# Attention query tiles, low products' chunks and attention output loaded earlier in a hybrid encoder block

## The chip, the cores and the metric

The kernel runs on one core of a Trainium2 chip. The core's engines are TensorE (PE in the profile: matrix products into PSUM, the matmul accumulators), VectorE (DVE), ScalarE (ACT), GpSimd (POOL) and SyncE (SP, which here only issues transfers); transfers between device memory and the on-chip SBUF run on 16 DMA engines, and their issues stand in the instruction queue of SP or POOL in program order. The metric is the time of one execution in microseconds (us) on the device; less is better.

## The reference

One layer for 1024 tokens of width 1024, all in float32:

```python
h = rms_norm(x, norm_mix)
proj = h @ w_in                    # q, k, v | rwkv columns | gates
attn = windowed_gqa(rope(norm(q)), rope(norm(k)), v, sink)   # 8 heads, 2 kv heads, +-128 tokens
zr = zr + shift_mu * (centred_shift(zr) - zr)
rw = rwkv7_time_mix(zr, ...)       # 8 heads of 64, one forward and one backward scan, summed
gates = sigmoid(proj[..., O_GATE:])
merged = gates[0] * (attn @ w_up_attn) + gates[1] * (rw @ w_up_rwkv)
x = x + merged @ w_out
x = x + square(relu(rms_norm(x, norm_ffn) @ w_ff1)) @ w_ff2
x = x + (p @ w_ple) * sigmoid(rms_norm(x, norm_ple) @ w_ple_gate)
```

In the scan each head holds a 64x64 state that is updated token by token with state·w + (state·a) b^T + v k^T; the output is state·r.

## The kernel before

Every float32 product of the large kind is made of three matmuls: each operand is split into a high part (a cast on ACT, line 198) and a low part (a subtraction on DVE or POOL, line 199), and high·high, low·high and high·low are summed. `split` does this, `mm3_steps` issues the three matmuls, one a step.

The work runs in stages. From 0 to 100 us: norm and the q, k, v projections (q and k go to device memory, `qT_d`, `kT_d`). From 100 to 280 us: the preparation of the scan in four channel groups of 128 (p = 0..3) and two directions; decay and in-context-rate products (`low_rank`, with the weights `wlr_h[0]`, `wlr_h[1]`, `wlr_l`), and the results written out as `ra_d`, `bk_d` (operands in chunks of 64 tokens), `v_d` and `bv_d` (the bonus term, tile `bv`, made from the PSUM tile `px`). From 280 to 340 us: the gate products of the first 512 tokens (`gates0`, tiles `gmm`: 16 gates of 24 matmuls) fill PE; their weights come as tiles `wst` on SP. From 340 to 476 us: windowed attention in 8 blocks of 128 queries (scores `sc`, transposes `pt`, outputs `po`, written to `at_d`), with the rest of gates0 as filler of low priority. From 476 to about 770 us: the scan, 16 steps of 64 tokens in both directions at once; then the up-projections, `w_out`, the FFN and the last embedding product, which the change does not touch.

A scan step s needs its operands (`rac`, `bkc`), its values (`UV`), the chunk products `gps` (`products`, evicted by DVE into the tile `gm`), sums (`sps`, `wy`, `ups`, `wa`) and transposes (`tmps`). Steps come in blocks of four. For each block a 64x64 triangular matrix per head and chunk has to be inverted: `low_products` loads pieces `la`, `lb` of `ra_d` and `bk_d` for its four chunks and multiplies them (`lps`); DVE then runs 31 pairs of vector operations (`inverse_steps`, tiles `tmp` and `Z`) to `Zn`, and PE turns the result into the inverse with `qps`. All this for block b+1 takes place during block b. The four chunks of low products are called in the first step of a block, one at each of four places; each call loads the chunk after it.

The scan's matmuls are issued in the order of the code (`mmo` pins it). Between them stand gaps: `fill(n)` takes n steps from one stream of filler, `beside()`: first the gate products of the last 512 tokens (`gates(1, ...)`), then the attention's up-projection (`uaps`: 8 groups of 12 matmuls for each half of the tokens), for which the attention output `at_d` is loaded (tile `atl`) and split into `aTh` and `aTl`. Between the two streams of filler stand `BRIDGE` = 26 empty steps, in which a gap issues nothing. Ahead of the scan a scheduler orders the matmuls by priority; it also places DMA issues on SP and POOL, and a pool of tiles that reuses the room of an earlier pool makes its first writers wait for that pool's last users.

SBUF room is handed from stage to stage: the attention's own pool `A2` opens on room that the preparation has used, and its query tiles `qT` (POOL, line 899), band masks `band` (line 903) and `sink` (line 905) are loaded there.

## Time and profile before

| | |
|---|---|
| three runs | 1707.08, 1701.10, 1699.73 us; median 1701.10 |
| the profiled execution | 1696.2 us, its span 1694.4 us |
| PE busy | 1615.2 us (95%) |
| DVE, ACT, POOL busy | 1138.1, 847.0, 103.1 us |
| mean granted TensorE clock | 0.982 of full speed |
| DMA | 269.23 MB, mean 159 GB/s |

The profile is a page on one execution and a trace that can be asked for more. A wait row reads: engine, tile and line that waited, what released it, then the total in us, the times and the longest. A window row gives the length, the busy time of PE, PE's weight loads, DVE, ACT and POOL with the number of instructions, then the granted TensorE clock (1.00 is full speed), the busy share of the DMA engines and GB/s. A row of the chain or of the timeline gives the start, the duration, the engine and the line; in brackets stands the idle time before it and what ended it. A row of groups gives line, engine, operation, tiles and count, then the total, the mean in ns, and the idle time before them.

### The profile page before, as it was taken

The page shows a single profiled execution, that of the slowest core. Times are in us where ns is not written, and L with a number is a line of the kernel's source. Part 1 is how long each engine was busy: PE and PEld are TensorE (multiplying, and loading weights), DVE is VectorE, ACT ScalarE, POOL GpSimd, SP SyncE. Part 2 cuts the span into 40 slices and gives each one's busy share as a digit, 9 for nine tenths or more (in the row PEclk, how much of TensorE's full clock was granted, in tenths as well). Part 3 has the DMA queues.
Part 4 walks back from the last instruction along what each step waited for, and adds up shares of the span by engine and source line. Part 5 has one row for each costly group of instructions (what it writes and reads, how often), then busy time and mean ns, then how long its engine had stood idle before and what let it go on. Part 6 is the DMA issues. An engine that isn't in the chain of part 4 may idle for free.

```text
span 1694.4 us, 31186 instructions
## 1 busy us (share of the span) xinstructions
PE 1615.2 (95%) x12280; PEld 1311.1 (77%) x12280; DVE 1138.1 (67%) x2055; ACT 847.0 (50%) x1537; POOL 103.1 (6%) x113
## 2 busy tenths in 40 slices
PE   7999999989999999698999999999999999999998
PEld 7987777856667787565778878888888888888887
DVE  6648998255948686775854887666767867685342
ACT  5558887357754544365423455444445444554121
POOL 3430000321200000000000000000000000000000
PEclk9999999989999999799999999999999999999999
DMA  6363556755366554446652154444449865574110
GB/s 222 82 154 106 161 172 174 229 171 152 104 181 182 159 162 129 154 150 217 232 195 95 55 174 150 155 147 164 143 150 345 286 200 166 155 219 145 41 41 38
DMA packets 200834, 269.23 MB, mean 159 GB/s; under 512 B 47728, under 2 KB 103920, under 8 KB 200688
## 3 DMA queue, kind: packets, MB, share of 16 engines
q1 hardware_dynamic: 190752, 254.14, 47.3%
q0 software_dynamic: 9792, 12.59, 2.9%
q8 instruction: 96, 1.57, 0.4%
q10 hardware_dynamic: 144, 0.52, 0.1%
q14 instruction: 50, 0.41, 0.1%
HBM read 186.45 MB, written 80.74 MB: 158 GB/s over the span
## 4 chain that ended last, share of the span: by engine, by line
PE 74%; DVE 11%; DMA 6%; ACT 4%; issue 3%; POOL 1%; SPq 0%; DVEq 0%; ACTq 0%; POOLq 0%
PE ff2ps L1856 17%; PE ff1ps L1604 16%; PE gmm L221 4%; PE uaps L221 2%; PE plps L231 2%; PE plps L229 2%; PE plps L227 2%; PE mm L239 2%; PE mm L241 2%; PE mm L240 2%; PE gps L221 1%; DMA wst<-in_w_col_dram 1%; DMA g1t<-g_d 1%; PE mmo L241 1%; PE mmo L239 1%
## 5 line engine op out<-in xcount | busy, mean ns | idle before, releaser
L1856 PE MATMUL ff2ps<-tl,sh 128*128 128x512 f32 x448 | 174.5, 389 | 0.1
L1856 PE MATMUL ff2ps<-th,sl 128*128 128x512 f32 x448 | 174.4, 389 | 0.0
L1856 PE MATMUL ff2ps<-th,sh 128*128 128x512 f32 x448 | 174.0, 389 | 0.0
L198 ACT CAST sh<-sst 128x512 fp32r<-128x512 f32 x109 | 67.7, 622 | 106.4 <-PE ff2ps L1856 59.9
L199 DVE TENSOR_TENSOR sl<-sst,sh 128x512 fp32r<-128x512 f32 x109 | 75.2, 690 | 46.5 <-ACT sh L198 46.1
L1604 PE MATMUL ff1ps<-mh,w1h 128*128 128x512 f32 x256 | 100.3, 392 | 1.9 <-ACT w1h L198 1.9
L1604 PE MATMUL ff1ps<-ml,w1h 128*128 128x512 f32 x256 | 99.9, 390 | 0.0
L1604 PE MATMUL ff1ps<-mh,w1l 128*128 128x512 f32 x256 | 99.6, 390 | 0.0
L1856 PEld LDWEIGHTS ff2ps<-tl,sh 128*128 128x128 f32 x448 | 84.1, 188 | 17.9 <-DVE tl L199 0.5
L1856 PEld LDWEIGHTS ff2ps<-th,sh 128*128 128x128 f32 x448 | 84.0, 188 | 17.8 <-ACT th L198 0.3
L1856 PEld LDWEIGHTS ff2ps<-th,sl 128*128 128x128 f32 x448 | 84.1, 188 | 17.6
L198 ACT CAST whi<-wst 128x512 fp32r<-128x512 f32 x100 | 60.4, 617 | 73.4 <-DMA wst<-in_w_col_dram 30.7
L183 POOL TENSOR_TENSOR rstd<-ms,neghalf 128x1 f32<-128x1 f32 x24 | 14.8, 616 | 1031.8 <-PE ff2ps L1856 572.7
L198 ACT CAST w1h<-w1st 128x512 fp32r<-128x512 f32 x48 | 28.3, 620 | 98.4 <-DMA w1st<-in_w_ff_dram 60.8
L199 DVE TENSOR_TENSOR w1l<-w1st,w1h 128x512 fp32r<-128x512 f32 x48 | 31.7, 688 | 53.1 <-ACT w1h L198 53.1
L199 DVE TENSOR_TENSOR wlo<-wst,whi 128x512 fp32r<-128x512 f32 x72 | 48.1, 688 | 19.9 <-ACT whi L198 19.5
L227 PE MATMUL gmm<-hh,whi 128*128 128x512 f32 x136 | 56.2, 413 | 3.6 <-ACT whi L198 3.6
L1604 PEld LDWEIGHTS ff1ps<-mh,w1h 128*128 128x128 f32 x256 | 48.1, 188 | 12.9 <-ACT w1h L198 2.8
L1604 PEld LDWEIGHTS ff1ps<-mh,w1l 128*128 128x128 f32 x256 | 48.1, 188 | 10.9 <-DVE w1l L199 0.6
L229 PE MATMUL gmm<-hl,whi 128*128 128x512 f32 x136 | 55.9, 411 | 0.0
L1604 PEld LDWEIGHTS ff1ps<-ml,w1h 128*128 128x128 f32 x256 | 48.1, 188 | 10.0
L231 PE MATMUL gmm<-hh,wlo 128*128 128x512 f32 x136 | 55.3, 408 | 0.0
(403 smaller groups left out, 4544.0 us busy)
## 6 DMA issues: line engine op xcount, KB each, us to landing
wst<-in_w_col_dram SPq DMA_DIRECT2D x92, 256.0 KB, 3.5
tst<-in_w_ff_dram SPq DMA_DIRECT2D x80, 256.0 KB, 4.1
w1st<-in_w_ff_dram SPq DMA_DIRECT2D x32, 512.0 KB, 5.0
hid_S<-h SPq DMA_DIRECT2D x64, 256.0 KB, 2.1
sst<-hid_S SPq DMA_DIRECT2D x64, 256.0 KB, 3.0
hid_A<-h SPq DMA_DIRECT2D x48, 256.0 KB, 2.0
sst<-hid_A SPq DMA_DIRECT2D x45, 256.0 KB, 3.8
ra_d<-ra SPq DMA_DIRECT2D x8, 1024.0 KB, 5.7
```

Source lines behind the costliest of these rows:

```text
L183: nc.gpsimd.tensor_tensor(out=r, in0=ms, in1=neghalf.broadcast_to([P, width]), op=ALU.pow)
L198: a = nc.scalar.copy(hi, src)
L199: b = (lo_eng or nc.vector).tensor_tensor(out=lo, in0=src, in1=hi.bitcast(F32), op=ALU.subtract)
L221: tc.keep_in_program_order(nc.tensor.matmul(*a, **kw))
L227: mm(ps, ah, bh, start=(i == 0), stop=False)
L229: mm(ps, ah, bl, start=False, stop=False)
L231: mm(ps, al, bh, start=False, stop=(i == n - 1))
L239: nc.tensor.matmul(ps, ah, bh, start=(i == 0), stop=False)
L240: nc.tensor.matmul(ps, ah, bl, start=False, stop=False)
L241: nc.tensor.matmul(ps, al, bh, start=False, stop=(i == n - 1))
L1604: nc.tensor.matmul(ps, x_[:, k, :], y_[:, k, :], start=start and k + i == 0, stop=k == 3 and i == 2, skip_group_check=True)
L1856: nc.tensor.matmul(banks[bs][i], x_[:, isl], y_, start=fresh and p + j == 0, stop=p == NPR - 1 and j == 2, skip_group_check=True)
```

## The change

It has four parts.

1. The low-rank weights move into a pool `q0` of their own, whose three tags are then reused: the query tiles take turns in the room of `wlr_h[0]` and `wlr_h[1]`, and band and sink share one tile in that of `wlr_l`. The first two query tiles, band and sink are loaded right behind the last low-rank products, ahead of `kT`, instead of at the attention's start. The pool is closed after the attention.
2. `low_products` gets the pool for `la` and `lb` and a number `ahead`: 2 in the attention, 3 in the scan. ahead − 1 chunks are loaded before the first product, and the next load is issued before a chunk's matmuls, not behind them, so there are three sets of tiles instead of two in the scan.
3. The attention output is loaded ahead, into the last 4 KB of each partition of the two `gm` tiles (1024 of 4096 elements, which `gm` leaves free). The first half's four loads stand at the start of the filler stream, with the first two `w_up_attn` weights; the second half's stand right behind the splits of the first, and its splits (`part`) are spread over the last group of the first half. The weights are prefetched across the two halves.
4. `BRIDGE` goes from 26 to 6.

On PE, around the attention's first score matmuls (`sc`); `gmm` is the filler of gates0. Before:

```order
L231 MATMUL gmm<-hh_92,wlo 128x512
L227 MATMUL gmm<-hh_92,whi 128x512
L928 MATMUL sc<-kT,qT 128x256 x4
L229 MATMUL gmm<-hl_93,whi 128x512
L231 MATMUL gmm<-hh_92,wlo 128x512
L928 MATMUL sc<-kT,qT 128x256 x2
```

Now:

```order
L229 MATMUL gmm<-hl_93,whi 128x512
L231 MATMUL gmm<-hh_92,wlo 128x512
L934 MATMUL sc<-kT,qT 128x256 x4
L227 MATMUL gmm<-hh_92,whi 128x512
L229 MATMUL gmm<-hl_93,whi 128x512
L231 MATMUL gmm<-hh_92,wlo 128x512
```

The four sc stood 60 gmm behind the last four px matmuls of the preparation; they now stand 20 gmm behind them, and 25 gmm follow before the next sc, where 2 did. In both programs the first sc also waits for DVE's bv, the last reader of px, whose PSUM room the score tile takes.

On SP, in the last step of the scan that makes low products: `la` and `lb` in groups of four issues are chunks, the `rac`, `bkc` and `UV` the next steps' operands, `g_d` a gate's result written out, `wst` a gate's weights. Before:

```order
L884 DMA rac_3039<-ra_d 128x512
L884 DMA rac_3036<-ra_d 128x512
L782 DMA la<-ra_d 128x4x64
L783 DMA lb<-bk_d 128x4x64
L782 DMA la<-ra_d 128x4x64
L783 DMA lb<-bk_d 128x4x64
L330 DMA g_d<-gth 128x512
L782 DMA la<-ra_d 128x4x64
L783 DMA lb<-bk_d 128x4x64
L782 DMA la<-ra_d 128x4x64
L783 DMA lb<-bk_d 128x4x64
L1151 DMA UV<-v_d 64x512 x2
```

Now:

```order
L895 DMA rac_3049<-ra_d 128x512
L895 DMA rac_3046<-ra_d 128x512
L793 DMA la<-ra_d 128x4x64
L794 DMA lb<-bk_d 128x4x64
L793 DMA la<-ra_d 128x4x64
L794 DMA lb<-bk_d 128x4x64
L330 DMA g_d<-gth 128x512
L215 DMA wst<-in_w_col_dram 128x512 x2
L1177 DMA UV<-v_d 64x512 x2
```

Before, the third and the fourth chunk stand here; now only the fourth, at the third's place, and the third has moved ahead by one group.

On PE, in the last step of the third block: `tmps` are the next step's transposes and `qps` the turn of the last inverse. Before:

```order
L1159 MATMUL tmps<-ident,bkc_3038 128x128 x4
L1159 MATMUL tmps<-ident,bkc_3041 128x128 x4
L221 MATMUL qps<-Zn,lt 32x32 x64
L221 MATMUL uaps<-aTh,wuhi 128x512
L221 MATMUL uaps<-aTl,wuhi 128x512
L221 MATMUL uaps<-aTh,wulo 128x512
```

Now:

```order
L1185 MATMUL tmps<-ident,bkc_3048 128x128 x4
L1185 MATMUL tmps<-ident,bkc_3051 128x128 x4
L221 MATMUL uaps<-aTl,wuhi 128x512
L221 MATMUL uaps<-aTh,wulo 128x512
L221 MATMUL uaps<-aTh,wuhi 128x512
L221 MATMUL uaps<-aTl,wuhi 128x512
L221 MATMUL uaps<-aTh,wulo 128x512
L221 MATMUL qps<-Zn,lt 32x32 x64
```

With 13 more between the sums of this step (8 ahead of `sps`, 5 ahead of `tmps`), 18 uaps now stand ahead of these qps, where none did, and 8 instead of 6 behind them. The 20 are gone from the end of the stream, the last two gaps ahead of the second up-projection's operands.

The diff, cut where it only renames:

```diff
@@ -55,7 +55,7 @@
 
 GATT = 1
 
-BRIDGE = 26
+BRIDGE = 6
 FILL = (5, 5, 3, 5, 3, 2, 4, 1)
 FILLEND = 2
 
@@ -512,6 +512,8 @@
         return pc[:, PC[name] + j:PC[name] + j + 1]
 
 
+    sQ0 = ExitStack()
+    Q0 = pool(sQ0, "q0", side="right")
     with ExitStack() as s1:
         A1 = pool(s1, "prep")
...
@@ -537,8 +539,8 @@
         nc.vector.tensor_scalar_mul(hka, pc[:, PC["k_a"]:PC["k_a"] + 4], 0.5)
         nc.vector.tensor_scalar(out=oka, in0=hka, scalar1=-1.0, scalar2=1.0, op0=ALU.mult, op1=ALU.add)
 
-        wlr_h = [A1.tile([P, ND, 512], F32R, name=f"wlrh{i}") for i in range(2)]
-        wlr_l = A1.tile([P, ND, 512], F32R, name="wlrl")
+        wlr_h = [Q0.tile([P, ND, 512], F32R, name=f"wlrh{i}", tag=f"q{i}", bufs=1) for i in range(2)]
+        wlr_l = Q0.tile([P, ND, 512], F32R, name="wlrl", tag="q2", bufs=1)
         hrows, lrows = [slice(0, 64), slice(64, 128)], [slice(64, 128), slice(0, 64)]
         for i in range(2):
             st = A1.tile([P, ND, 512], F32, name="wlrst", tag="th", bufs=3)
@@ -748,12 +750,21 @@
                 ops = normed_keys(p + 1, *nxt)
 
         kT = PY.tile([P, 2, 2, T], F32R, name="kT", tag="yk")
+        qT0 = Q0.tile([P, NH, P], F32R, name="qT", tag="q0", bufs=1)
+        nc.gpsimd.dma_start(qT0, qT_d[0])
+        bands = Q0.tile([P, 3 * P + NH], F32, name="band", tag="q2", bufs=1)
+        band = bands[:, 0:3 * P].rearrange("p (b t) -> p b t", b=3)
+        nc.sync.dma_start(band, I["band"])
+        sink = bands[:, 3 * P:]
+        nc.sync.dma_start(sink, I["qkn"][:, 640:648].partition_broadcast(P))
         for q in range(4):
             ts = slice(256 * q, 256 * q + 256)
             a = nc.gpsimd.dma_start(kT[:, :, :, ts], kT_d[:, :, :, ts])
             if q:
                 after(a, on_pool[0])
             fill0(NP - 1, 1)
+        qT1 = Q0.tile([P, NH, P], F32R, name="qT", tag="q1", bufs=1)
+        nc.gpsimd.dma_start(qT1, qT_d[1])
         for _ in bonus:
             pass
 
@@ -773,10 +784,10 @@
         nc.gpsimd.memset(z[64:96, :, 32:64], 0.0)
         return z
 
-    def low_products(pl, ps_of, b, mm, behind=None):
+    def low_products(pl, po, ahead, ps_of, b, mm, behind=None):
 
         def load(ci):
-            la, lb = ([pl.tile([P, NP, 64], F32, name=n, bufs=4) for _ in range(ND)] for n in ("la", "lb"))
+            la, lb = ([po.tile([P, NP, 64], F32, name=n, bufs=2 * ahead) for _ in range(ND)] for n in ("la", "lb"))
             for d in range(ND):
                 c = chunk(NB * b + ci, d)
                 for a in (nc.sync.dma_start(la[d], ra_d[d, c][:, :, 0:64]),
@@ -785,11 +796,13 @@
                         after(a, behind)
             return la, lb
 
-        nxt = load(0)
+        nxt = [load(ci) for ci in range(ahead - 1)]
         yield
         lt = pl.tile([P, 32, 64], F32, name="lt", bufs=1)
         for ci in range(NB):
-            la, lb = nxt
+            if ci + ahead - 1 < NB:
+                nxt.append(load(ci + ahead - 1))
+            la, lb = nxt.pop(0)
             pss = [ps_of([P, NP, 64], "lps") for _ in range(2)]
             for j in range(NP):
                 for q in range(2):
@@ -800,8 +813,6 @@
                         mm(pss[e][own[d], j, :], l_[d][rows, j, :], r_[d][rows, j, :], start=True, stop=True)
             for e in range(2):
                 nc.scalar.copy(lt[:, 8 * ci + e:8 * ci + 8:2, :], pss[e])
-            if ci + 1 < NB:
-                nxt = load(ci + 1)
             yield lt
 
     def inverse(pl, lt):
@@ -895,22 +906,17 @@
             return PA.tile(shape, F32, name=name, tag="tp", bufs=3)
 
         def queries(n):
-            qT = A2.tile([P, NH, P], F32R, name="qT", bufs=2)
+            qT = Q0.tile([P, NH, P], F32R, name="qT", tag=f"q{n % 2}", bufs=1)
             nc.gpsimd.dma_start(qT, qT_d[n])
             return qT
 
-        band = A2.tile([P, 3, P], F32, name="band")
-        nc.sync.dma_start(band, I["band"])
-        sink = A2.tile([P, NH], F32, name="sink")
-        nc.sync.dma_start(sink, I["qkn"][:, 640:648].partition_broadcast(P))
-        qT0 = queries(0)
         V = A2.tile([P, NT, P], F32, name="V")
         nc.sync.dma_start(V, va_d.rearrange("(t q) c -> q t c", q=P))
         A3 = A2
         nsink = A3.tile([P, NH], F32, name="nsink")
         nc.vector.tensor_scalar_mul(nsink, sink, -1.0)
         for n in range(NT):
-            qT = queries(n) if n else qT0
+            qT = queries(n) if n > 1 else (qT0, qT1)[n]
             k0, k1 = max(n - 1, 0), min(n + 2, NT)
             nk = k1 - k0
             b0 = k0 - (n - 1)
@@ -959,7 +965,7 @@
             nc.scalar.copy(at, po)
             put = nc.sync.dma_start(at_d[:, :, n * P:(n + 1) * P], at)
             if n == 0:
-                low0 = low_products(BI, ps_att, 0, nc.tensor.matmul, put)
+                low0 = low_products(BI, A2, 2, ps_att, 0, nc.tensor.matmul, put)
                 next(low0)
             if n == 1:
                 zi = zi_tile(BI, "zi")
@@ -975,6 +981,7 @@
                 pass
             for _ in gates(1, range(GATT)):
                 pass
+    sQ0.close()
     y = PY.tile([P, NP, T], F32, name="y", tag="yk")
 
 
@@ -983,39 +990,56 @@
     sR, sU, sC, sRB = (ExitStack() for _ in range(4))
     epi = {}
     def beside():
+        def load_at(h):
+            for k in range(NP):
+                nc.sync.dma_start(epi["at"][k], at_d[:, k, 512 * h:512 * h + 512])
+
+        def load_wu(pl, m):
+            st = pl.tile([P, NP, P], F32, name="wust", tag="wu_st", bufs=2)
+            nc.sync.dma_start(st, I["w_up_attn"][m])
+            return st
+
+        load_at(0)
+        sts = [load_wu(B, m) for m in range(2)]
         yield from gates(1, range(GATT, 2 * KT), mmo, lo_of=lambda m: nc.vector)
         sW.close()
         sH1.close()
         epi["RWA"] = pool(sR, "rwA", side="right")
         UA = epi["UA"] = pool(sU, "ua", side="right")
+        aTh = UA.tile([P, NP, 512], F32R, name="aTh", tag="aTh", bufs=1)
+        aTl = UA.tile([P, NP, 512], F32R, name="aTl", tag="aTl", bufs=1)
+
+        def weights(m, st=None):
+            hi = UA.tile([P, NP, P], F32R, name="wuhi", tag="wu_hi", bufs=3)
+            lo = UA.tile([P, NP, P], F32R, name="wulo", tag="wu_lo", bufs=3)
+            split(hi, lo, st or load_wu(UA, m))
+            return hi, lo
+
+        def part(k):
+            split(aTh[:, k, :], aTl[:, k, :], epi["at"][k])
+
+        ahead = [weights(0, sts[0])]
+        for k in range(NP):
+            part(k)
+        load_at(1)
+        ahead.append(weights(1, sts[1]))
+        for _ in range(BRIDGE):
+            yield 1
         for h in range(2):
             hs = slice(512 * h, 512 * h + 512)
-            aTh = UA.tile([P, NP, 512], F32R, name="aTh", tag="aTh", bufs=1)
-            aTl = UA.tile([P, NP, 512], F32R, name="aTl", tag="aTl", bufs=1)
-            for k in range(NP):
-                at = UA.tile([P, 512], F32, name="atl", tag="mgt", bufs=2)
-                nc.sync.dma_start(at, at_d[:, k, hs])
-                split(aTh[:, k, :], aTl[:, k, :], at)
-            def weights(m):
-                st = UA.tile([P, NP, P], F32, name="wust", tag="wu_st", bufs=2)
-                nc.sync.dma_start(st, I["w_up_attn"][m])
-                hi = UA.tile([P, NP, P], F32R, name="wuhi", tag="wu_hi", bufs=3)
-                lo = UA.tile([P, NP, P], F32R, name="wulo", tag="wu_lo", bufs=3)
-                split(hi, lo, st)
-                return hi, lo
-
-            ahead = [weights(0), weights(1)]
-            if h == 0:
-                for _ in range(BRIDGE):
-                    yield 1
             for m in range(KT):
                 hi, lo = ahead.pop(0)
-                if 0 < m < KT - 1:
-                    ahead.append(weights(m + 1))
+                if (h, m) != (0, 0) and (h, m) < (1, KT - 1):
+                    ahead.append(weights((m + 1) % KT))
                 g = UA.tile([P, 512], F32, name="gta", tag="g1t", bufs=2)
                 nc.sync.dma_start(g, g_d[m, :, hs])
                 ps = PMM.tile([P, 512], F32, name="uaps", tag="mm", bufs=2)
-                yield from mm3_steps(ps, [(hi[:, k, :], lo[:, k, :], aTh[:, k, :], aTl[:, k, :]) for k in range(NP)], mmo)
+                for j, _ in enumerate(mm3_steps(ps, [(hi[:, k, :], lo[:, k, :], aTh[:, k, :], aTl[:, k, :]) for k in range(NP)], mmo)):
+                    if (h, m) == (0, KT - 1) and j and j % 3 == 0:
+                        part(j // 3 - 1)
+                    yield
+                if (h, m) == (0, KT - 1):
+                    part(NP - 1)
                 nc.vector.scalar_tensor_tensor(out=g, in0=g, scalar=1.0, in1=ps, op0=ALU.add, op1=ALU.mult)
                 nc.sync.dma_start(mg_d[m, :, hs], g)
                 yield
@@ -1106,7 +1130,9 @@
     AC = [PH0, None]
     B = pool(sC, "chunks")
 
-    gm = [AC[0].tile([P, NB, 2, 6, 64], F32, name=f"gm{hf}", tag=f"ab{hf}", bufs=1) for hf in range(2)]
+    gms = [AC[0].tile([P, 4096], F32, name=f"gm{hf}", tag=f"ab{hf}", bufs=1) for hf in range(2)]
+    gm = [g[:, 0:3072].rearrange("p (n e a t) -> p n e a t", n=NB, e=2, a=6) for g in gms]
+    epi["at"] = [gms[k // 2][:, 3072 + 512 * (k % 2):3584 + 512 * (k % 2)] for k in range(NP)]
 
     ch_tm, ch_uv, ch_wy, Sc = {}, {}, {}, {}
 
@@ -1282,7 +1308,7 @@
             next(inv[0], None)
 
     def begin_low(b):
-        lows[b] = low_products(BI, ps_gps, b, mmo)
+        lows[b] = low_products(BI, B, 3, ps_gps, b, mmo)
         next(lows[b])
 
     def end_inverse(b, between):
```

## The prediction

> **What bounds the kernel now.** I read the page first, for which engine carries the span; then the waits of the TensorE (PE), for where it stands still; then 10-us windows around those waits, for how long it stands and how slow it is afterwards; last the chain of waits and single rows, for what is late next.
>
> ```profile
> span 1694.4 us, 31186 instructions
> PE 1615.2 (95%) x12280; PEld 1311.1 (77%) x12280; DVE 1138.1 (67%) x2055; ACT 847.0 (50%) x1537; POOL 103.1 (6%) x113
> PE lps L221 <- DMA lb<-bk_d: 8.8, 3, 4.0
> PE sps L221 <- ACT UV L1211: 7.4, 2, 6.6
> PE sc L928 <- DMA qT<-qT_d: 6.8, 1, 6.8
> PE uaps L221 <- ACT aTh L198: 5.5, 2, 4.8
> PE qps L221 <- DVE Zn L1274: 4.9, 1, 4.9
> PE gps L221 <- DVE gm L1142: 2.1, 1, 2.1
> ```
>
> PE is busy 95% of the span, so time is won only where it stands idle (79 us in all) or runs at a lower granted clock. Each wait row gives the total, the count and the longest one. Parts of the change aim at lps, sc, uaps and at the stretch with sps and qps. PE's matmul count stays at its size and the stages from the FFN on are untouched, so everything below is about some 50 us of idle and slow time between 280 and 820 us. In a window row the idle time is the length less PE's first number, and the loss to the clock is that busy time times (1 − PEclk).
>
> **Part 1, query tiles and bands early.** In the program before, the first score matmuls stand 60 filler matmuls (gmm) behind the last px group, and wait for qT.
>
> ```profile
> 326.14 0.39 PE L618 MATMUL px<-s2l,one_r 128*128 128x512 f32 x1
> 326.37 0.39 PE L229 MATMUL gmm<-hl,whi 128*128 128x512 f32 x1
> 326.60 0.39 PE L231 MATMUL gmm<-hh,wlo 128*128 128x512 f32 x1
> 334.74 1.29 DVE L636 TENSOR_TENSOR bv<-px,z 128x512 f32<-128x512 f32 x2 [22.37 <-DMA v_d<-vt]
> 347.33 1.19 PE L928 MATMUL sc<-kT,qT 128*128 128x256 f32 x4 [6.76 <-DMA qT<-qT_d]
> 349.28 0.17 DVE L911 TENSOR_SCALAR nsink<-sink 128x8 f32<-128x8 f32 x1 [13.25 <-DMA sink<-in_qkn_dram]
> 340.00:350.00 10.00, 2.60 (x9) 1.48 (x7) 0.71 (x4) 1.73 (x3) 5.22 (x6) 0.68 0.95 291
> 350.00:360.00 10.00, 9.98 (x46) 8.51 (x47) 6.69 (x29) 6.53 (x24) 0.61 (x2) 0.81 0.39 133
> ```
>
> These 20 us hold 7.4 us idle and 2.6·0.32 + 10·0.19 = 2.7 us of slow clock. Now the first sc stands only 20 gmm behind px (the order shown with the change), and filler starts every 0.23 us: PE reaches it at 326.4 + 20·0.23 = 331.0. Its score tile takes the PSUM room of px, and px is read by bv, which ended at 334.74 + 1.29 = 336.0. So the wait for qT (6.8) becomes one for bv (5.0), and the stall goes from 7.4 to 5.0: a gain of 2.4, with the clock loss as before since the gap is still long. The 40 fillers that the wait jumps over are not lost; they move into the attention and to its end. Between 0 (the attention is set by DVE, filler or not) and 4 more could come from that; I take 1.
>
> The price is paid earlier. qT0 and qT1 (512 KB each) and the band (192 KB) now enter at about 280.5, ahead of two weight tiles (wst) that the gates' filler needs.
>
> ```profile
> 282.00:288.00 6.00, 6.00 (x28) 4.81 (x27) 5.54 (x5) 4.61 (x7) 0.78 (x1) 1.00 0.97 277
> 288.00:294.00 6.00, 2.48 (x12) 1.49 (x10) 2.29 (x4) 1.97 (x4) 0.00 (x0) 0.87 0.89 233
> 286.46 6.96 DMA wst<-in_w_col_dram
> ```
>
> There the DMA engines are 97% busy at 277 GB/s, and PE already idles 3.5 us for wst. 1.24 MB more at 277 GB/s is 4.5 us; if the added loads fill only gaps, the cost is 0. With a share of 0.97 the upper end is the nearer: I take 3.5. The Trainium skill ("DMA: Bandwidth & Descriptors", Issuing engines are not separate DMA queues) says that loads issued on POOL share the 16 engines with SP's and only save issue time; by that the cost is the full 4.5 us, whereas a path of its own for POOL would leave the band's 0.7 us. No run here shows which. Part 1 in all: 2.4 + 1 − 3.5 = **0** (−4 to +6).
>
> Two waits are added in front of others. On POOL the two qT loads wait for the low-rank products' matmuls, with the kT loads and POOL's weight splits behind them; nothing asks for kT before the first sc 50 us later, so that costs nothing. On SP the four loads of the attention output's first half wait for the last matmul of the first gates, since their room is the filler's operands; behind them stand wst, and the first scan step's bkc, rac and UV. At this handover DVE also has four weight splits (wlo) between Zn and the first gm, where gps already waited 2.1.
>
> ```profile
> L199 DVE TENSOR_TENSOR wlo<-wst,whi 128x512 fp32r<-128x512 f32 x72 | 48.1, 688 | 19.9 <-ACT whi L198 19.5
> ```
>
> Four at 0.69 us are 2.8, and a wst that comes late through SP's wait would add to them; 24 filler matmuls (5.5 us) now stand ahead of gps and hide most. I take **−1.5** (−3 to 0).
>
> **Part 2, the low products' chunks a place earlier.** In three steps of the scan, four steps apart, the last of four chunks of low products stalls PE, because its lb was issued too late.
>
> ```profile
> 500.00:510.00 10.00, 7.31 (x201) 5.94 (x192) 3.10 (x5) 8.68 (x21) 0.00 (x0) 1.00 0.61 153
> 510.00:520.00 10.00, 9.99 (x197) 8.27 (x201) 6.38 (x16) 3.33 (x8) 0.00 (x0) 0.83 0.74 213
> 570.00:580.00 10.00, 7.87 (x205) 6.51 (x195) 3.79 (x6) 8.33 (x20) 0.00 (x0) 0.96 0.63 155
> 580.00:590.00 10.00, 10.00 (x227) 8.27 (x220) 6.85 (x18) 3.89 (x9) 0.00 (x0) 0.87 0.80 219
> 640.00:650.00 10.00, 6.05 (x148) 4.86 (x150) 4.11 (x10) 6.64 (x17) 0.00 (x0) 0.87 0.60 155
> 650.00:660.00 10.00, 10.00 (x195) 8.29 (x194) 6.31 (x16) 3.36 (x8) 0.00 (x0) 0.79 0.44 137
> 506.02 3.86 DMA lb<-bk_d
> ```
>
> For the last of the three steps, SP's la issues (in a question of that line for 636 to 638 and for 642 to 644 us) show the places:
>
> ```profile
> L782 SPq DMA_DIRECT2D la<-ra_d x2: 558/934/1309, 636.4 to 637.7; - x2
> L782 SPq DMA_DIRECT2D la<-ra_d x1: 1722/1722/1722, 642.4 to 642.4; - x1
> ```
>
> Idle: 2.69 + 2.13 + 3.95 = 8.8, the three waits. Clock: 1.7 + (0.3 + 1.3) + (0.8 + 2.1) = 6.2. With the third set of tiles the last chunk's four loads stand on SP's queue where the third's stood, from 636.4 instead of 642.4, 6 us earlier; the longest wait was 4.0 and a load lands in 3.9 us, so the wait is gone, and DVE (6.4 of 10 us busy) has room to follow. The whole is 15.0; if short gaps elsewhere take a fifth of it back, 12. I take **14**.
>
> The Trainium skill ("TensorE: Matmul & The Clock Gate", Part 1: The HAM clock gate) lets the clock fall to half only after an idle window of about 3.4 us. By that rule only the third stall has a clock loss, and the term is 8.8 + 2.9 = 11.7. The trace speaks against it: after the 2.1 us of 570:580 the clock was 0.87.
>
> **Part 3, attention output and first weights ahead; BRIDGE 26 to 6.**
>
> ```profile
> 680.00:690.00 10.00, 7.11 (x210) 5.76 (x208) 5.88 (x17) 2.26 (x4) 0.00 (x0) 1.00 0.77 231
> 690.00:700.00 10.00, 4.13 (x68) 3.91 (x68) 7.83 (x18) 5.39 (x9) 0.00 (x0) 0.66 0.79 259
> 700.00:710.00 10.00, 5.08 (x136) 4.70 (x135) 9.73 (x19) 5.15 (x10) 0.00 (x0) 0.60 0.29 92
> 686.56 4.50 DMA atl<-at_d
> 692.45 3.56 DMA atl<-at_d
> 703.48 1.98 DVE Zn L1274
> L199 DVE TENSOR_TENSOR aTl<-atl,aTh 128x512 fp32r<-128x512 f32 x4 | 2.8, 693 | 5.8 <-ACT aTh L198 5.7
> ```
>
> Idle is 13.7 us and the clock costs 1.4 + 2.0 here. ACT sits in order: the UV copy that sps waits for stands behind casts that wait for atl; DVE loses 5.8 us to the same, and Zn, which qps waits for, is late by it. With the halves already in SBUF the DMA waits go. What is late next is DVE: all four aTl and two wulo still stand ahead of the last inverse pairs, and two or three more ops of 0.7 us stand there than before. So Zn comes 5.8 − 2.5 = about 3 us earlier, not 6, and PE still waits before qps. Into that wait go 18 more uaps (18·0.23 = 4.2 us), 20 with the two behind it. They leave the last two gaps before gps in front of the second up-projection, where DVE makes its operands and is 9.6 of 10 us busy (810:820, quoted last); PE arrives 4.7 us earlier there and waits perhaps 3 of it back. So 3 + 1.7 and about 1.3 of clock: **6** (2 to 11). If cover there is wholly gone, the 20 matmuls bring nothing.
>
> **Part 4, the second half.**
>
> ```profile
> 770.00:780.00 10.00, 4.08 (x13) 2.25 (x12) 6.11 (x10) 4.41 (x8) 0.00 (x0) 0.85 0.83 283
> 780.00:790.00 10.00, 9.72 (x33) 7.20 (x33) 5.48 (x9) 5.40 (x8) 0.00 (x0) 0.80 0.76 234
> 772.53 5.59 DMA atl<-at_d
> 810.00:820.00 10.00, 10.00 (x44) 7.86 (x43) 9.62 (x15) 5.30 (x8) 0.00 (x0) 1.00 0.80 276
> ```
>
> Idle 6.2, clock 0.6 + 1.9 = 2.5: 8.7 together. The second half is loaded some 80 us before its use, and its eight splits of 0.6 to 0.7 us are spread over the preceding group of 12 matmuls (2.8 us), so a remainder of a few splits may show: **8** (5 to 9).
>
> **Sum.** 0 − 1.5 + 14 + 6 + 8 = 26.5 us. The profiled execution took 1696.2 us with its span of 1694.4, so it would become 1669.7. The runs' median, 1701.1, lies 4.9 above it; on that scale the forecast is 1674.6, rounded **1675**.
>
> **Rivals.** (A) All of it goes: Zn comes the full 6 us early and the tail keeps the 4.7 (6 more), the early loads cost nothing (3.5 more) and the filler closes the attention's gaps (3 more): 39 gained, **1662**. For it: DVE still idles 4 us in 680:690. Against: the share of 0.97 above, and DVE's 9.73 in 700:710.
> (B) Only Part 2 works. The early loads cost 4.5 and the attention gives back nothing of it, the handover costs 3, the first half moves from waiting on atl to waiting on DVE and the tail takes back the 4.7, and of Part 4 only 3 are left: 14 − 4.5 + 2.4 − 3 + 0 + 3 = 12, with Part 2 at its low end 8: **1692**. For it: every stall of Part 3 sits beside a nearly full DVE.
> (C) Part 2 does not do what it says, because SP reaches the loads no sooner: SP works in order, and g_d or wst waits ahead of them may hold it. Then 26.5 − 14 = 12.5 is left: **1689**. Against it: before, SP issued the third chunk's loads from 636.4 at the place the last one now takes.
> (D) Slower. SP stands still at the new place: the last chunk's loads now overwrite the first chunk's tiles and wait for its matmuls; if SP gets there first, the next step's rac, bkc and UV loads queue behind them, and that step starts late by up to a step's length, in three blocks. Steps last about 17 us (the three stalls, four steps apart, lie 70 us apart). At 13 us a block it costs 39, 12.5 net of the gains: **1713**. It decides from 26.5/3 = 9 us a block. Against it: before, the third chunk's loads stood at this place with the same condition, and were out from 636.4 on.
>
> **How the numbers follow.** A measurement of this kernel tells about 0.5% (8.5 us) from no change. Forecast 0.55, A 0.12, B 0.20, C 0.05, D 0.08. The range 1655 to 1696 leaves out D and a little of B and A. Half of B lies within 8.5 us of 1701: faster is 0.55 + 0.12 + 0.04 + 0.09 = 0.80, same 0.11 + 0.01 = 0.12, slower 0.08.
>
> **What would show it.** Part 1: the first sc starts near 336 plus the delay of wst, released by DVE's bv; the gap at 289 to 294 grows by 0 to 4.5 us. Part 2: no wait of lps on lb above 0.5 us, and PE at 10 of 10 at full clock in those six windows. Part 3: sps no longer waits 6.6, qps still waits on Zn, mups or mmc waits more on rwl. Part 4: no wait of uaps on aTh. The forecast is wrong if the wait for gps at the handover exceeds 5 us, if a new wait on rac, bkc or UV shows in the scan, or if part of the 14 comes back as short waits on DVE.

## The result and the profile after

The changed kernel takes 1684.22 us, the median of four runs (1681.88 to 1685.89); four runs of the kernel before beside it have a median of 1700.41 (1698.2 to 1707.08). The ratio is 0.9897, with a 95% interval of 0.9866 to 0.9929: 12 to 23 us faster. The forecast was 1675 with a range of 1655 to 1696. The direction and the range held; of the 26.5 us of gain about 16 came, and not where most of them were forecast.

The profile page of the changed kernel (first lines), to be set beside the span of 1694.4 us before:

```profile
span 1684.1 us, 31165 instructions
PE 1615.9 (96%) x12280; PEld 1307.8 (78%) x12280; DVE 1134.6 (67%) x2055; ACT 844.5 (50%) x1535; POOL 103.1 (6%) x113
```

The rows of PE's waits between 280 and 830 us of the changed kernel that matter here (what waited, what released it; total, count, longest):

```profile
PE gmm L227 <- ACT whi L198: 4.6, 1, 4.6
PE qps L221 <- DVE Zn L1300: 4.3, 1, 4.3
PE sc L934 <- DVE bv L638: 4.3, 1, 4.3
PE pt L955 <- DVE smk L952: 4.1, 3, 2.0
PE mups L221 <- ACT rwh L198: 3.8, 3, 2.4
PE uaps L221 <- ACT aTh L198: 3.7, 1, 3.7
PE wy L221 <- issue: 3.5, 2, 2.2
PE lps L221 <- ACT lt L815: 3.1, 2, 1.7
PE gps L221 <- DVE gm L1168: 1.5, 2, 1.2
```

Of the rows of before, lps on lb (8.8), sps on UV (7.4) and sc on qT (6.8) are gone from the scan and the attention's start. In their place stand sc on bv, as forecast, and others that were not forecast: lps on lt (ACT's copy of an earlier chunk's products), wy on "issue" (the profile shows nothing that PE waited for; 1.5 before), pt on smk in the attention (a product that waits for DVE; 1.5 before), and a uaps wait that moved forward from the second half of the attention output to the first. The longest wait, gmm on whi, is that of the gates for a weight tile at 288 to 294 us (3.6 before, in two).

Windows of the changed kernel, columns as before (length, PE, PEld, DVE, ACT, POOL, then clock, DMA share, GB/s):

```profile
288.00:294.00 6.00, 1.52 (x9) 1.05 (x7) 1.60 (x3) 1.34 (x2) 0.00 (x0) 0.91 1.11 350
500.00:510.00 10.00, 7.48 (x170) 5.91 (x169) 4.12 (x7) 6.33 (x14) 0.00 (x0) 1.00 0.76 231
510.00:520.00 10.00, 9.01 (x152) 7.31 (x153) 4.38 (x11) 6.14 (x16) 0.00 (x0) 0.83 0.78 211
560.00:570.00 10.00, 7.78 (x234) 6.75 (x233) 4.39 (x9) 4.05 (x7) 1.11 (x2) 0.80 0.29 84
570.00:580.00 10.00, 10.00 (x231) 7.87 (x231) 2.92 (x6) 6.74 (x16) 0.00 (x0) 0.86 0.42 108
580.00:590.00 10.00, 9.23 (x203) 7.20 (x200) 4.37 (x9) 7.20 (x19) 0.00 (x0) 1.00 0.89 217
640.00:650.00 10.00, 10.00 (x288) 8.12 (x277) 4.58 (x10) 9.05 (x22) 0.00 (x0) 1.00 0.63 157
650.00:660.00 10.00, 9.28 (x229) 7.33 (x221) 6.18 (x16) 5.07 (x13) 0.00 (x0) 1.00 0.45 140
680.00:690.00 10.00, 6.15 (x201) 4.84 (x199) 5.55 (x15) 2.95 (x7) 0.00 (x0) 0.95 0.72 220
690.00:700.00 10.00, 9.89 (x90) 7.69 (x90) 9.14 (x24) 5.50 (x11) 0.00 (x0) 0.71 0.63 192
700.00:710.00 10.00, 5.70 (x134) 5.01 (x133) 9.62 (x16) 4.49 (x8) 0.00 (x0) 0.63 0.42 130
757.10:802.30 45.20, 39.61 (x326) 28.98 (x327) 34.69 (x60) 31.50 (x48) 0.00 (x0) 1.00 0.73 235
```

The last window reaches from the sums (sps) of step 14, the last of the scan's steps that can be told apart in this way, to the first matmul of the second up-projection (mmc). For it, and for one window that the prediction had no reason to show, the kernel before has:

```profile
560.00:570.00 10.00, 9.14 (x340) 7.49 (x342) 3.28 (x7) 5.07 (x11) 1.10 (x2) 1.00 0.42 124
757.90:812.60 54.70, 46.62 (x345) 34.19 (x346) 35.65 (x62) 32.58 (x49) 0.00 (x0) 0.94 0.66 210
```

In this tail idle time went from 8.1 to 5.6 us and busy time from 46.6 to 39.6: 20 uaps fewer (102 for 122, 4.7 us; the windows count 19) and a clock of 1.00 in place of 0.94. In the second profile of the same program, introduced next, the clock is 0.96 there. From mmc to the end both profiles take 881.8 us, so the whole difference of the spans lies before it. The places where sps of a step starts, and mmc, give an account by stretch. The second profile is that of another execution of the same changed program (the fifth experiment below), with a span of 1679.2 us:

| stretch | before, us | changed, us | again, us | forecast | changed | again |
|---|---|---|---|---|---|---|
| to sps of step 0 (Part 1, handover) | 503.7 | 504.0 | 502.3 | +1.5 | +0.3 | -1.4 |
| step 0 to step 10 (Part 2) | 172.9 | 171.6 | 169.8 | -14 | -1.3 | -3.1 |
| step 10 to step 14 (Part 3) | 81.3 | 81.5 | 78.7 | -4.3 | +0.2 | -2.6 |
| step 14 to mmc (Part 4, 20 uaps) | 54.7 | 45.2 | 46.6 | -9.7 | -9.5 | -8.1 |
| sum | 812.6 | 802.3 | 797.4 | -26.5 | -10.3 | -15.2 |

One program differs by 4.9 us from one profile to the next. The changed kernel's own profiled execution (1685.89 us) was the slowest of its four runs and the one of before (1696.2) lay 4 us below its median; that is why the profiles show 10.3 us and the medians 16.2. In both profiles the tail has what was forecast, and the scan up to step 10 has a tenth to a fifth of it.

### The profile page after: what moved, and what is told of

It reads as the page before. It is cut to its first block, busy times and chain, and to the rows that moved or that the text cites. A ratio compares the mean times of both kernels' runs of the same rounds, so it can differ in the third digit from the quotient of the medians.

```text
span 1684.1 us, 31165 instructions
## 1 busy us (share of the span) xinstructions
PE 1615.9 (96%) x12280; PEld 1307.8 (78%) x12280; DVE 1134.6 (67%) x2055; ACT 844.5 (50%) x1535; POOL 103.1 (6%) x113
## 4 chain that ended last, share of the span: by engine, by line
PE 74%; DVE 10%; DMA 6%; ACT 5%; issue 3%; POOL 1%; SPq 0%; DVEq 0%; ACTq 0%; POOLq 0%
PE ff2ps L1882 18%; PE ff1ps L1630 16%; PE gmm L221 4%; DMA wst<-in_w_col_dram 2%; PE plps L231 2%; PE plps L229 2%; PE plps L227 2%; PE mm L239 2%; PE mm L240 2%; PE mm L241 2%; PE uaps L221 1%; PE gps L221 1%; PE mmo L241 1%; PE mmo L239 1%; PE mmo L240 1%
## 5 line engine op out<-in xcount | busy, mean ns | idle before, releaser
L199 DVE TENSOR_TENSOR wlo<-wst,whi 128x512 fp32r<-128x512 f32 x72 | 47.9, 687 | 29.5 <-ACT whi L198 29.4
```

The source lines that it names most:

```text
L199: b = (lo_eng or nc.vector).tensor_tensor(out=lo, in0=src, in1=hi.bitcast(F32), op=ALU.subtract)
```

## The experiments

Each was timed beside the kernel before on the same chip; ratios are to that, with 95% intervals. The experiments ran on three chips, so where two variants did not run side by side the ratios are the fairer comparison. Ten runs of the changed program in two sets spread from 1679.75 to 1686.57, so differences of 3 or 4 us between two variants are not resolved, and what a stretch of one profile shows is read with the 4.9 us above in mind.

**Part 1 undone.** The query tiles, band and sink load again at the attention's start, into rooms of their own; the other parts stay.

```diff
-        wlr_h = [Q0.tile([P, ND, 512], F32R, name=f"wlrh{i}", tag=f"q{i}", bufs=1) for i in range(2)]
+        wlr_h = [A1.tile([P, ND, 512], F32R, name=f"wlrh{i}") for i in range(2)]
...
-        nc.gpsimd.dma_start(qT0, qT_d[0])
...
+        qT0 = queries(0)
```

> The changed kernel with part 1 undone: low-rank weights back in the preparation's pool, the query tiles, band and sink loaded at the attention's start; parts 2, 3 and 4 stay. Theory A (the attention is paced by DVE and its filler stands in a fixed order, so an earlier start only moves PE's idle time into the attention): 0 to 2 us slower than the changed kernel, first score matmuls near 347 us again, but the scan's first gps within 1 us of the changed kernel's 473.8. Theory B (the earlier start is kept, 4 to 5 us of stall and slow clock): 4 to 5 us slower, first gps near 478.

Measured: 1681.64 us (1679.34 to 1689.92), ratio 0.9903 (0.9882 to 0.9923), against 0.9897 with Part 1. Its wait for qT is back at 6.5 us and the first sc at 347.5 in place of 336.4, yet the time is that of the changed kernel within what can be told. Its profile is that of its slowest run, and there the first gps comes at 476.4 (changed: 473.8) and step 0 at 508.2. By the times Part 1 as it stands is worth about nothing, as forecast. The one profile does not settle it: its gps, 2.5 us later, lies between the 1 and the 4 us of the two expectations.

**Part 2 undone.** Two sets of la and lb tiles again, the next chunk loaded behind a chunk's matmuls.

```diff
-        lows[b] = low_products(BI, B, 3, ps_gps, b, mmo)
+        lows[b] = low_products(BI, ps_gps, b, mmo)
...
+            if ci + 1 < NB:
+                nxt = load(ci + 1)
```

> The changed kernel with part 2 undone: low products' chunks loaded one ahead in two sets, as before; parts 1, 3 and 4 stay. Theory A (ACT, which works in order and evicts each chunk's products with 2.3 us of copies beside the gate weights' casts, takes the place of the late loads): 4 to 7 us slower than the changed kernel. Theory B (as forecast, the three stalls and their slow clock are all won): 12 to 15 us slower. In both the three waits of lps on lb return with 2 to 4 us each.

Measured: 1685.85 us (1683.52 to 1687.39), ratio 0.9916 (0.9900 to 0.9932): 1.6 us above the changed kernel, which is not resolved and is less than either expectation (4 to 7, 12 to 15). Two rows of its PE waits:

```profile
PE lps L221 <- DMA lb<-bk_d: 8.3, 3, 3.0
PE wy L221 <- issue: 1.0, 2, 0.8
```

The three waits for lb return at nearly their old size, and the time hardly moves. Part 2 removes them and pays for it nearly as much elsewhere. By steps (the time from one sps to the next): with Part 2, steps 5 and 9 take 16.7 and 16.2 us in place of 17.8 and 20.9, 5.8 less; steps 1, 4, 8 and 11 take 20.5, 26.4, 23.0 and 18.6 in place of 19.4, 22.5, 21.8 and 17.1, 7.7 more. The next sections follow these.

**bv in a room of its own.** The bonus term of the last channel group no longer waits for the room of vt, which is being written out (the 22.4 us on v_d in the row of bv that the prediction shows).

```diff
-            bv = A1.tile([P, T], F32, name="bv", tag="vt", bufs=1)
+            bv = A1.tile([P, T], F32, name="bv", tag="rk" if p == NP - 1 else "vt", bufs=1)
```

> The changed kernel, and the last group's bonus tile bv takes the room of rk (which its sums have read by then) instead of that of vt, so that it need not wait until vt is written out. Both theories: the 4.3 us wait of the first score matmuls on bv goes, and they start near 332 instead of 336.4. Theory A (DVE's work in the attention and the weight splits behind it set when the scan starts): the scan's first gps moves by less than 2 us and the time by 0 to 2. Theory B (PE's stall is what counts): the time falls by 4 to 5.5 us, stall and slow clock.

Measured: 1678.77 us (1675.33 to 1680.91), ratio 0.9874 (0.9855 to 0.9893). The fall of 5.4 us is what the second expectation named, and three of its four runs lie below the lowest of ten runs of the changed program; but those did not run beside it and the intervals of the ratios overlap. A later experiment tests the edit side by side. The wait of sc for bv is gone, the first sc starts at 328.5 in place of 336.4, the first gps at 466.8 in place of 473.8. But step 0 starts at 500.6, only 3.4 us earlier: a new wait of its own stands in between.

```profile
PE gmm L221 <- ACT gth L329: 4.3, 1, 4.3
```

A gate's result gth sits behind two casts on ACT that wait for a late weight tile wst. Of 7 us at the attention's end about half survive to the first step.

**First up-projection weight off the gates' room.** In the changed kernel the first wuhi lies in the room of the last gate's gth, and its cast waits until that gate is written out. Here the first gta tile of the up-projection, which is needed later, takes that room first.

```diff
+        g0 = UA.tile([P, 512], F32, name="gta", tag="g1t", bufs=2)
         ahead = [weights(0, sts[0])]
...
-                g = UA.tile([P, 512], F32, name="gta", tag="g1t", bufs=2)
+                g = UA.tile([P, 512], F32, name="gta", tag="g1t", bufs=2) if (h, m) != (0, 0) else g0
```

> The changed kernel, and the up-projection's pool places its gta tiles first, so that the first up-projection weights no longer take the room of the last gate's result, whose writing out they waited for (2.85 us on ACT, 4.1 on DVE). Theory A (this wait took the place of the wait for the attention output): the casts start at 686 instead of 688.9, Zn 2.5 to 3 us earlier than 702.4, PE's wait for Zn 4.3 shrinks as well, and the time falls by 2.5 to 4 us with the clock. Theory B (DVE is full there and Zn hardly moves): 0 to 1 us.

Measured: 1682.98 us (1680.3 to 1685.63), ratio 0.9899 (0.9880 to 0.9918), no difference that can be told, as the second expectation had it. The timelines show what happened, first ACT's, PE's and DVE's rows of the changed kernel:

```profile
688.91 0.62 ACT L198 CAST wuhi<-wust 128x512 fp32r<-128x512 f32 x1 [2.85 <-DMA g_d<-gth]
690.10 0.80 PE L221 MATMUL uaps<-aTh,wuhi 128*128 128x512 f32 x1 [3.74 <-ACT aTh L198]
702.44 2.05 DVE L1300 STREAM_TRANSPOSE Zn<-Z 128x1024 f32<-128x1024 f32 x1
704.64 2.58 PE L221 MATMUL qps<-Zn,lt 32*32 32x32 f32 x89 [4.30 <-DVE Zn L1300]
```

and PE's rows with the edit:

```profile
686.50 0.50 PE L221 MATMUL uaps<-aTh,wuhi 128*128 128x512 f32 x1 [1.05 <-ACT aTh L198]
701.65 2.58 PE L221 MATMUL qps<-Zn,lt 32*32 32x32 f32 x89 [5.54 <-DVE Zn L1301]
```

The cast's wait for a write-out goes, uaps starts 3.6 us earlier and step 11 takes 15.7 in place of 18.6 us; then qps waits for Zn 1.2 us longer. So the wait for the loads of atl, which the change removed, had come back in the changed kernel as a wait for the store g_d, and behind it qps still waits for DVE's Zn. Steps 11 and 12 together take 45.0 us here, 47.9 in the profile of the changed kernel and 45.1 in the second profile of the same program, where the cast's wait for the store was 0.9 us: the gain is no larger than the spread of one program.

**The changed kernel again**, the same program, beside the next two.

> The changed kernel itself once more, beside the next ones. Open is the gap in PE's instruction stream (released by issue) right behind the second block's inverse, near 567 us: 2.2 us in the changed kernel, 2.5 and 2.2 in two of its variants, but 0.4 in the one with bv in another room, 0.9 before the change and 0.8 with part 2 undone. If it belongs to the program it is 2.0 to 2.5 again and the step it lies in lasts about 26 us; if it changes from one execution to the next it can come out near 0.5, and that step then lasts 22 to 23 us. Time 1680 to 1686.

Measured: 1683.55 us (1679.75 to 1686.57), ratio 0.9906 (0.9884 to 0.9929). Its profile is the last column of the table above. The gap near 567 us was 1.9 us and its step took 25.0, nearer to what was expected if the gap belongs to the program.

**The second half loaded late.** The loads of the attention output's second half stand again at the start of that half in the code, but keep their own room.

```diff
-        load_at(1)
         ahead.append(weights(1, sts[1]))
...
+            if h:
+                load_at(1)
+                for k in range(NP):
+                    part(k)
+                ahead = [weights(0), weights(1)]
```

> The changed kernel with part 4 undone: the second half of the attention output and its first two weights are loaded and split only when the first half's groups are through, its splits are not spread. Theory A (the second half is where the change's gain comes from, 10 us in the trace between the first epilogue and the last up-projection): 8 to 10 us slower than the changed kernel beside it, with a wait of uaps on aTh of 4 to 5 us near 760 us. Theory B (the gain there comes from the 20 filler matmuls that moved): 0 to 4 us slower.

Measured: 1685.56 us (1677.74 to 1688.16), ratio 0.9914 (0.9890 to 0.9938). It undid less than meant: SP still issued these loads at 691 to 695 us, since nothing holds them once their room is free. It left Part 4 undecided; the last experiment takes it up.

**One chunk ahead in the first block.** If the early la and lb issues on SP hold the gates' weights back, loading one chunk less ahead in block 1 should shorten step 1.

```diff
-        lows[b] = low_products(BI, B, 3, ps_gps, b, mmo)
+        lows[b] = low_products(BI, B, 2 if b == 1 else 3, ps_gps, b, mmo, sets=3)
```

> The changed kernel, but for the block whose low products fall into the scan's first step only one chunk is loaded ahead instead of two; the later blocks keep two. Theory A (at the scan's start the extra chunk's issues stand on SP ahead of the gate weights, wst comes late, and ACT waits for it with the products' evictions queued behind): wst is issued near 490 instead of 495 and 501, the two waits of lps on lt (3.1 us) shrink to under 1, and the step from 504 to 524 lasts 17.5 to 19 instead of 20.5 us: 1.5 to 4 us faster than the changed kernel beside it. Theory B (the copies of the products themselves are the limit): no change.

Measured: 1682.67 us (1679.34 to 1689.97), ratio 0.9903 (0.9879 to 0.9927). The weight tiles were issued at 490.7 and 500.2 us in place of 495.0 and 501.4, and step 1 took 20.3 us (changed: 20.5 and 20.8). Too little of the queue was moved for a test; the ninth experiment moves all of it.

**Three mends together**: the two room edits and the one just shown.

> The changed kernel with bv in rk's room, the first up-projection weights off the last gate's room, and one chunk ahead in the first block. If the three act at their own places, their single gains add: 5.4 + 1.5 to 3 + 1.5 to 4, so 8 to 12 us faster than the changed kernel beside it, 1672 to 1676. If DVE's work behind the attention and the inverse takes them back, no more than the 5 us that the first one alone brought.

Measured: 1685.31 us (1683.86 to 1686.43), ratio 0.9915 (0.9896 to 0.9935). The gains do not add, and with the edit of bv among them the time is no shorter than the changed kernel's beside it (1683.55): the wait of gmm for gth is 6.2 us, the first step starts at 509.9 us, and the wait for Zn is 5.9.

**The scan's la and lb loads on POOL's queue**, so that they no longer stand ahead of the gates' weights on SP.

```diff
-                for a in (nc.sync.dma_start(la[d], ra_d[d, c][:, :, 0:64]),
-                          nc.sync.dma_start(lb[d], bk_d[d, c][:, :, 64 * d:64 * d + 64])):
+                for a in (eng.dma_start(la[d], ra_d[d, c][:, :, 0:64]),
+                          eng.dma_start(lb[d], bk_d[d, c][:, :, 64 * d:64 * d + 64])):
...
+        lows[b] = low_products(BI, B, 3, ps_gps, b, mmo, eng=nc.gpsimd)
```

> The changed kernel, with the scan's la and lb loads issued on POOL's queue in place of SP's; rooms and order stay. Theory (the gain of Part 2 is spent at once: with a third set of tiles 16 more issues of 0.6 to 1.6 us stand on SP ahead of the gates' weight loads wst, whose landing in order holds whi on ACT and, behind it, the eviction lt that lps waits for): wst of the first block comes back from about 495 and 501 us to 481 to 491, the waits of lps on ACT lt go, the first step of a block falls from 20.5 to 17.5 to 18 us, and the time by 2.5 to 3.5 us a block where this showed, 3 to 8 us in all: about 1676 to 1681. Rival (the transfers share the DMA engines whichever queue issues them, or POOL's own weight splits now stand in front of the loads): lb comes late again, waits of lps on lb of 1 to 3 us return, and the time is 1683 to 1690.

Measured: 1687.88 us (1684.29 to 1691.37), ratio 0.9920 (0.9894 to 0.9945). This is the chain it was to break, in SP's, ACT's and PE's rows of the changed kernel:

```profile
495.00 1.17 SPq L215 DMA_DIRECT2D wst<-in_w_col_dram  x2
501.44 0.85 SPq L215 DMA_DIRECT2D wst<-in_w_col_dram  x2
506.78 0.62 ACT L198 CAST whi<-wst 128x512 fp32r<-128x512 f32 x1 [3.19 <-DMA wst<-in_w_col_dram]
507.72 0.33 PE L221 MATMUL lps<-lb,la 64*64 64x64 f32 x2 [1.66 <-ACT lt L815]
```

Before, these weight issues stood at:

```profile
484.19 1.01 SPq L215 DMA_DIRECT2D wst<-in_w_col_dram  x2
491.87 0.93 SPq L215 DMA_DIRECT2D wst<-in_w_col_dram  x2
```

ACT works in order: whi waits 3.2 us for the late wst, the eviction lt of the finished low products stands behind it, and the next lps needs the room that lt frees. With the loads on POOL, the weights are issued at 486.9 and 494.9, the waits of lps for lt are gone, and step 1 takes 17.9 us in place of 20.5, as the theory had it. Yet the time is not 3 to 8 us less: the ratio is 2 to 4 us above that of the changed kernel, which is not resolved. In the profile the scan's first step comes 4.9 us later (step 0 at 508.9). The windows and two rows show the place:

```profile
482.00:484.00 2.00, 1.36 (x20) 0.80 (x13) 0.00 (x0) 1.59 (x3) 0.00 (x0) 1.00 1.08 260
484.00:486.00 2.00, 0.00 (x0) 0.00 (x0) 0.00 (x0) 0.00 (x0) 0.00 (x0) 0.73 1.00 287
486.00:488.00 2.00, 1.44 (x3) 1.16 (x4) 0.00 (x0) 0.00 (x0) 0.00 (x0) 0.50 1.06 383
486.56 0.79 PE L221 MATMUL gmm<-hl,whi 128*128 128x512 f32 x1 [3.20 <-issue]
```

For two microseconds none of PE, DVE, ACT and POOL works while the transfers are at full share; PE resumes with an idle time of 3.2 us that no semaphore explains, and then at half clock. The theory about the queue held for the first step, and its price was wrong. The rival, that the transfers share the DMA engines, names the time (1683 to 1690) but not the way: no lb came late in the scan.

**The same with bv in its own room.**

> The kernel with the low products' loads on POOL's queue, and bv of the last pair in a room of its own as in the run with that single edit. If the two gains are of different places they add: about 4 to 5 us below the run with the POOL loads alone, near 1673 to 1677. If the start of the attention is only traded against filler that then lacks later, it is at most 1 us below that run. The first sc starts near 328 in either case, and the wait of gmm on ACT gth (4.3) shows in either case.

Measured: 1679.32 us (1676.35 to 1682.75), ratio 0.9869 (0.9842 to 0.9895): 8.6 us below the run before it on the same chip, and no run of the one lies in the range of the other. So on top of the POOL loads the edit of bv is a real gain, larger than the 4 to 5 us expected, though the time is above the 1673 to 1677 named. In the profiles step 0 comes 4.0 us earlier (505.0 against 508.9); where the rest comes from is not shown. The wait of gmm for gth, expected in either case, does not show in it. But it is no faster than the bv edit alone (1678.77).

**And with the first weight off the gates' room.**

> As the kernel before it in this list, with the first wuhi's room taken off the last gate's gth, so that its cast no longer waits for a write-out of the gates. If the waits are of separate places: step 11 falls from about 18.6 to 15.7 us, 1 to 4 us less than with the two edits: 1670 to 1675. If the gain goes into waits of qps on Zn and of the gates on gth, as it did with the three edits together in the earlier run, no less than with two: 1676 to 1684.

Measured: 1681.58 us (1679.38 to 1684.16), ratio 0.9886 (0.9861 to 0.9910). Nothing is gained: step 11 was already at 14.6 us without the edit, and qps now waits 9.1 us for Zn, with step 12 at 34.1 us in place of 29.7. This is the second of the two expectations.

**Part 4 undone through the old room.** The second half goes again through the two tiles atl and is split at its start; no weights ahead across the halves.

```diff
-        load_at(1)
...
+            if h:
+                for k in range(NP):
+                    at = UA.tile([P, 512], F32, name="atl", tag="mgt", bufs=2)
+                    nc.sync.dma_start(at, at_d[:, k, hs])
+                    split(aTh[:, k, :], aTl[:, k, :], at)
```

> The changed kernel, with the second half of the attention output loaded through the two-tile room and split between the halves as in the kernel before, and without the weights that were loaded ahead across the halves; the first half stays as changed. Theory (the gain that is seen lies in the tail, where the second half already stands in SBUF): a wait of uaps on aTh of 4 to 5 us returns near 760 to 780 us, the way from the start of step 14 to the second up-projection grows from 45 to 50 to 54 us, and the time is 5 to 9 us longer: 1689 to 1693. Rival (the tail's gain is that of the 20 matmuls moved into the bridge alone): the wait returns, but the way grows by 0 to 3 us and the time by at most 3: 1683 to 1687.

Measured: 1689.03 us (1681.93 to 1690.93), ratio 0.9919 (0.9892 to 0.9947). By the ratios that is 2 to 4 us above the changed kernel, which is not resolved. The window from step 14 to mmc:

```profile
755.00:806.30 51.30, 43.74 (x326) 32.13 (x327) 35.02 (x59) 31.78 (x47) 0.00 (x0) 0.90 0.66 220
```

The stretch is 51.3 us in place of 45.2, within the 50 to 54 of the theory. The wait for aTh in it did not come back: since the first half no longer uses these tiles, the first of the loads was out at 687.6, and the splits ran from 755 to 763 us, ahead of need. The 6.1 us are 2.0 of idle time, most of it a wait of the scan's own ups for DVE (1.7), and 4.1 of busy time at a clock of 0.90 in place of 1.00. That these belong to Part 4 is not shown. The twelve other profiles of the changed kernel and its variants have 44.6 to 50.3 us in this stretch, and the longest, the run with the loads on POOL, has Part 4 untouched:

```profile
754.29:804.55 50.26, 43.89 (x327) 32.19 (x327) 34.92 (x60) 31.74 (x47) 0.00 (x0) 0.90 0.64 215
```

The same low clock comes there without the edit. Neither the theory nor the rival had the wait stay away, and what Part 4 alone is worth stays open.

## Why the prediction was right or wrong

The direction and the range were right, the size by term was not. The range reached up to 1696, a gain of 5 us, so a time inside it says little for the terms and owes something to luck; with the largest of them nearly gone, the time lies nearer to rival C's 1689 and B's 1692 than to the forecast's 1675.

**Part 1 (0, of 2.4 + 1 - 3.5).** The sum was right, its terms were not. As forecast, the first sc waited for bv: 4.3 us, forecast 5.0, starting at 336.4. The price of the early loads was wrong: the gap at 288 to 294 grew from 3.5 to 4.5 us of idle time, so 1.0 and not 3.5 (0.7 in the second profile). In that window the transfers ran at 350 GB/s, after 233 before; a share of 0.97 at 277 GB/s was no limit. The rule that the prediction cited there from the Trainium skill ("DMA: Bandwidth & Descriptors", Issuing engines are not separate DMA queues) is not decided by this: the measured 1.0 us is nearer to the 0.7 named for a path of POOL's own than to the 4.5 of a shared one, but both supposed 277 GB/s, and the rate rose. What the wait gained was lost again in the attention: by its last scores it stood 6.3 us ahead of the kernel before (455.0 against 461.3), by the first gps 1.3 behind (473.8 against 472.5). The waits of pt for DVE, 4.1 us for 1.5, are part of that.

**The handover (1.5 later).** The wait of gps was 1.2 us instead of growing from 2.1, but gps came 1.3 us later, and step 0 0.3 later. Close, within one profile's spread.

**Part 2 (14).** This is the step that failed; it gave 1.3 and 3.1 us in the two profiles, and undoing it moved the time by 1.6. What was said of the loads held: no lps waits for lb in the scan, SP reached them earlier, and the second and third stall gave back 2.1 and 4.9 us against the kernel before (steps 5 and 9). What failed was "if short gaps elsewhere take a fifth of it back"; and the forecast took 14 where even that working gave 12. In the first profile the two steps gave 7.0 us, and steps 1, 4 and 8 took back 1.1, 3.9 and 0.6.

Three things took nearly all of it. First, 16 issues of la and lb, of 0.6 to 1.6 us each, now stand on SP between 476 and 500 us, ahead of or between the gates' weights, where four stood before; and through ACT's order these made a wait for lt out of the first wait for lb; step 1 grew by 1.1 us. That this is the cause of that wait, the run with the loads on POOL shows.

Second, step 4 grew from 22.5 to 26.4 us, by a stall on PE's instruction stream (last section): 2.2 us and a clock of 0.80 and 0.86 behind it, in windows where before it was 1.00 and 0.96. Whether Part 2 brings this stall on is not settled: of the twelve profiles with Part 2 eight have it at 1.7 us or more and four at 1.1 or less, and both without have the short one.

Third, a term of 6.2 us of the 15.0 was clock, on the ground that it comes back with the stall; in 510:520 it stayed at 0.83, with waits of only 1.7 and 1.4 us, ending at 507.7 and 511.0, whereas in 580:590, 640:650 and 650:660 it came back to 1.00. The clock rule of the Trainium skill that the prediction weighed ("TensorE: Matmul & The Clock Gate", Part 1: The HAM clock gate), with a fall only after 3.4 us of idle time, does not fit this 0.83 either; by it the term was 11.7, also too much. The sign that was named, PE at 10 of 10 at full clock in the six windows, did not come: it was 7.5 to 10.0 at 0.83 to 1.00.

**Part 3 (6).** The 20 uaps moved into the bridge and left the tail with 4.7 us less work, as said; no run puts BRIDGE back to 26, so this rests on the counts. The other 4.3, from waits in the bridge, failed at "with the halves already in SBUF the DMA waits go": the split's own output had been placed in room that a store still read, a wait of 2.85 us on g_d (0.9 in the second profile). Idle and slow time from 680 to 710 fell from 17.1 to 13.6 us, less than the 20 matmuls that were put there (11.7 in the second profile, which runs 3.5 us ahead). With that wait removed qps still waited for Zn on DVE, and the time did not fall by what can be told. Zn came at 702.4, 1.0 earlier, as step 10 did; in the second profile, counted from step 10, it came 1.9 earlier. It was not the 3 us that were allowed for.

**Part 4 (8, and 1.7 left of the 4.7).** Right in size as a sum: 9.5 and 8.1 us in the two profiles of the changed program, 4.4 to 10.1 over it and its variants. The split is not shown: if the tail kept the whole 4.7 of the matmuls, 3.4 to 4.8 are left for Part 4, below the 5 to 9 forecast. The wait on aTh for the second half went and the clock was 1.00 and 0.96; waits of mups (the means behind the scan) for rwh, the high part of their operand, took back part (3.8 us in the tail, 1.3 before).

**Rivals.** None happened as told. B had Part 2 as the only part that works; it was nearly the reverse. C was right that Part 2 would give almost nothing, and wrong about why: it had SP held up ahead of the low loads, where the low loads held SP. Its time, 1689, is 5 us off, the forecast's 9. A and D did not happen: the time is far from 1662 and from 1713, and no step of the scan waited for loads of rac, bkc or UV. The forecast's own sign for failure, that part of the 14 comes back as short waits on DVE, came true with ACT in DVE's place.

Not settled: why the same waits cost 6 us more or less from one variant to the next, apart from the instruction stream, and what Part 4 alone is worth. The best kernels seen are the change with bv in its own room (1678.8), and the same with the low loads on POOL (1679.3); one edit is the better choice.

## What to carry to other kernels

A load that is issued earlier is not only in time itself: all that stands behind it on its queue is later by the issue times, so name the next transfer in that queue and the engine that waits in order for it. When a wait goes, ask what room its successor is written to: a store that still reads the room makes the same wait again. And where several engines are within a few us of each other, add up gains per stretch of the timeline, not per wait; here waits worth 8.8 us left with 1 to 3 us of gain.
